# The recurrence's block-diagonal gate products: float32r in three passes instead of fp32

## The chip, the cores and the metric

The kernel runs on one NeuronCore of a Trainium2 chip. The metric is the device time of one execution in microseconds (us). The engines are named as the profile names them: PE (TensorE, matrix products; PEld is its loading of weights), DVE (VectorE), ACT (ScalarE), POOL (GpSimd) and SP (SyncE, which here issues DMA transfers). Lower is better.

## The reference, cut to what matters

The program is one inference step of a decoder layer on 264 tokens: 256 of a prompt and 8 single tokens of running sequences. A combined projection `xn @ w_in` feeds two groups of heads: a gated linear recurrence (RG-LRU) and an mLSTM. Then come an output projection, cross attention over 256 memory tokens, and a SwiGLU feed-forward part. The part that this document is about is the pair of gates of the recurrence:

```python
xr, conv_new = causal_conv(z[..., OFF_RGX:OFF_RGG], conv_buf, conv_w, conv_b)
r = jax.nn.sigmoid(block_diag(xr, w_rg_a, b_rg_a))
ig = jax.nn.sigmoid(block_diag(xr, w_rg_x, b_rg_x))
h_rg, h_last = rglru(xr, r, ig, rg_lambda, h0)
```

`xr` has 1024 channels in 8 blocks of 128. `block_diag` multiplies each block by a 128 x 128 matrix of its own, once for `r` and once for `ig`: 16 products of 128 x 128 by 128 x 264. From `r` and `ig` come the coefficients of a first-order recurrence over the 256 prompt tokens.

## The kernel before, in words

Activations lie transposed: channels on the 128 partitions, the 264 tokens along the free dimension. All large projections are a list of **steps** (`steps`, lines 164 and 1478). A step of the main kind takes one 128-column piece of a weight matrix (2048 rows, as 16 blocks of 128 x 128) and makes one 128 x 264 output in a PSUM bank.

**Three float32r passes.** Precision is kept by splitting each operand into a high part, rounded to float32r, and a low part, the rest. `mm3` (line 287) makes a product of three float32r passes: high by high, high by low, low by high. The moving operand is read in an order that interleaves its two halves (`turn`), and the result is read back the same way (`unturn`, `halves`). A step is so 16 x 3 = 48 passes. The weights are split while the kernel runs (`split_half`, line 183): a DMA on SP's queue brings half a step's weights (128 x 1024) into one of 5 `raw` tiles, ACT makes the high part, DVE subtracts it to make the low part, both into one of 4 `w` tiles, that is two steps' worth. These splits have a high priority.

**The order of the work.** Steps 0 to 3 are the first four projections of the recurrence's input, worked row by row; 4 to 7 the other four; 8 a narrow one for the mLSTM's gates (32 passes); 9 to 24 the mLSTM's q, k and v; 25 to 32 the recurrence's output gate; 33 to 40 the mLSTM's. Beside the list, **generators** make the work of the heads. After each step `pump` (line 323) lets each generator run until DVE's or ACT's clock, by the kernel's own prices, is ahead of PE's; `yield STEP` ends a generator's turn until the next step. What is issued so gets its priority from its place in the program, and a scheduler then orders each engine's queue by priority and by the time at which it reckons an operand ready; PE is ordered by hand only for steps 0 to 6 and at the end. Each engine works through its queue in that order.

**The recurrence's generator** is `rg_gen` (line 528), started at step 7. It loads the 16 gate matrices (two DMAs on SP's queue, 512 KB each), computes the decay's coefficients (`rg_coef`), and takes the 8 blocks in turn: `rg_conv(n)` (line 512) makes the causal convolution, one ACT instruction and three DVE instructions of some 256 to 296 columns and one short one. After every second block the generator ends its turn, and at its next it issues for both blocks the two gate products, in fp32, each followed by a sigmoid on ACT that reads the PSUM bank:

```python
            for q in (n - 1, n):
                for t, j, b in ((r, 0, "ba"), (ig, 1, "bx")):
                    ps = bank("ax")
                    pe.matmul(ps[:, :N], wr[j][:, q, :], rg["xr"](q), start=True, stop=True)
                    last = act.activation(t(q), ps[:, :N], AF.Sigmoid, bias=V(b, q))
```

Then come exponentials and square roots on ACT, multiplications and eight scans on DVE. Step 25 is not issued until `rg_gen` is through.

**Tiles.** Most intermediate tiles come from one pool of 26 slots (`B`, line 119): the normalized input (8 slots until step 40), the convolution's inputs, gate matrices, `xr`, `r`, `ig`, the mLSTM's tiles and loaded states.

**POOL** is used before the change for a few memsets, for DMA issue, and, in the cross attention, for low parts of 256 columns (lines 1202 and 1256).

Of the kernel before, what the change touches and what calls it, by code (L numbers as in the profile page):

```python
# [10 lines left out]
F32 = mybir.dt.float32  # L11
F32R = mybir.dt.float32r
I32 = mybir.dt.int32
AF = mybir.ActivationFunctionType
# [3 lines left out]
P = 128  # L18
# [4 lines left out]
N = T + NS  # L23
# [19 lines left out]
STEP = object()  # L43
# [52 lines left out]
def layer_kernel(ctx: ExitStack, tc, xT, memT, vec, wrg, w_in, w_out, w_q, w_k, w_v, w_o,  # L96
# [3 lines left out]
    act, dve, pe = Engine(nc.scalar, price_act), Engine(nc.vector, price_dve), Engine(nc.tensor, price_pe)  # L100
    pool_e, sp = nc.gpsimd, nc.sync
# [13 lines left out]
    def nm(s):  # L115
        uid[0] += 1
        return f"{s}_{uid[0]}"

    def B(shape, dt=F32):
        return sb.tile(shape, dt, tag="B", bufs=NB, name=nm("B"))  # L120

    def tmp(w=N, tag="t"):
        t = sb.tile([P, N], F32, tag=tag, bufs=NT if tag == "t" else NL, name=nm(tag))
        return t[:, :w]
# [146 lines left out]
    def by2(x):  # L271

        return x.rearrange("p (a b) -> p a b", b=2)

    def turn(x):

        return x.rearrange("p (b a) -> p a b", b=2)

    def halves(x):

        return x.rearrange("p (b a) -> p b a", b=2)

    def unturn(ps):

        return ps.rearrange("p (a b) -> p b a", b=2)

    def mm3(ps, a, b, start, stop):
        ah, al = a
        bh, bl = b
        ps, bh, bl = by2(ps), turn(bh), turn(bl)  # L290
        pe.matmul(ps, ah, bh, start=start, stop=False)
        pe.matmul(ps, ah, bl, start=False, stop=False)
        pe.matmul(ps, al, bh, start=False, stop=stop)
# [53 lines left out]
    def bank(tag="mm"):  # L347
        return psm.tile([P, 512], F32, tag=tag, bufs=4, name=nm(tag))
# [16 lines left out]
    def V(name, j=0, w=1):  # L365
        o = _V[name][0] + j
        return vecs[:, o: o + w]
# [87 lines left out]
    rg = {"zn": 0}  # L455

    def rg_coef():

        c = const.tile([P, 2 * RGB], F32, name="rgc")
        lam = V("lam", 0, 8)  # L460
        n_ = tmp(8)
        with tc.issue_after(st["low"].ins):
            dve.scalar_tensor_tensor(n_, lam, -1.0, lam, op0=OP.mult, op1=OP.min)
        e = tmp(8)
        act.activation(e, n_, AF.Exp)
        l1 = tmp(8)
        log1p(l1, e)
        m = tmp(8)
        dve.tensor_scalar(m, lam, -1.0, 0.0, op0=OP.mult, op1=OP.max)
        dve.tensor_add(m, m, l1)  # L470
        dve.tensor_scalar(c[:, :8], m, -8.0, None, op0=OP.mult)
        dve.tensor_scalar(c[:, 8:], m, -16.0, None, op0=OP.mult)
        rg["c"] = c

    def log1p(out, e):

        w = e.shape[-1]
        pp = e.shape[0]
        s = ctile(w)[:pp]
        q = ctile(w)[:pp]  # L480
        dve.tensor_scalar(q, e, 2.0, None, op0=OP.add)
        dve.reciprocal(q, q)
        dve.tensor_mul(s, e, q)
        s2 = ctile(w)[:pp]
        dve.tensor_mul(s2, s, s)
        dve.tensor_scalar(q, s2, 1.0 / 19, None, op0=OP.mult)
        for k in (17, 15, 13, 11, 9, 7, 5, 3):
            dve.scalar_tensor_tensor(q, q, 1.0 / k, s2, op0=OP.add, op1=OP.mult)
        dve.scalar_tensor_tensor(out, q, 1.0, s, op0=OP.add, op1=OP.mult)
        dve.tensor_scalar(out, out, 2.0, None, op0=OP.mult)  # L490
# [21 lines left out]
    def rg_conv(n):  # L512
        z = rg.pop(("z", n))
        zi, t = z[:, 0, :], z[:, 1, :]
        smp = zi[:, 267:299].rearrange("p (b j) -> p b j", j=4)
        act.activation(cpo[:, n, :], zi[:, 256:259], AF.Copy)
        act.activation(cso[:, n, :, :], smp[:, :, 1:4], AF.Copy)
        w = [V("cw", j * 8 + n) for j in range(4)]
        act.activation(t[:, :296], zi[:, 0:296], AF.Identity, scale=w[0], bias=V("cb", n))
        dve.scalar_tensor_tensor(t[:, :296], zi[:, 1:297], w[1], t[:, :296], op0=OP.mult, op1=OP.add)  # L520
        dve.scalar_tensor_tensor(t[:, :296], zi[:, 2:298], w[2], t[:, :296], op0=OP.mult, op1=OP.add)
        xr = rg["xr"](n)
        dve.scalar_tensor_tensor(xr[:, :T], zi[:, 3:259], w[3], t[:, :T], op0=OP.mult, op1=OP.add)
        ts = t[:, 267:299].rearrange("p (b j) -> p b j", j=4)
        dve.scalar_tensor_tensor(xr[:, T:N].rearrange("p (b j) -> p b j", j=1), smp[:, :, 3:4], w[3],
                                 ts[:, :, 0:1], op0=OP.mult, op1=OP.add)

    def rg_gen():
        wr = [B([P, 8, P]), B([P, 8, P])]
        for j in range(2):  # L530
            sp.dma_start(wr[j], wrg[:, j * 8: j * 8 + 8, :])
        rg_coef()
        r, ig = Arr(RGB), Arr(RGB)
        for n in range(RGB):
            while rg["zn"] <= n:
                yield STEP
            rg_conv(n)
            yield 1.5
            if n % 2 == 0:
                continue  # L540
            yield STEP
            for q in (n - 1, n):
                for t, j, b in ((r, 0, "ba"), (ig, 1, "bx")):
                    ps = bank("ax")
                    pe.matmul(ps[:, :N], wr[j][:, q, :], rg["xr"](q), start=True, stop=True)
                    last = act.activation(t(q), ps[:, :N], AF.Sigmoid, bias=V(b, q))
            yield 0.1
        yield STEP
        xr, c = rg["xr"], rg["c"]
        e2 = Arr(RGB)  # L550

        for n in range(RGB):
            with tc.issue_after(last.ins), tc.issue_after(st["split"].ins):
                act.activation(e2(n), r(n), AF.Exp, scale=c[:, 8 + n: 9 + n])
                le = act.activation(r(n), r(n), AF.Exp, scale=c[:, n: n + 1])
                act.activation(e2(n), e2(n), AF.Relu, scale=-1.0, bias=ones[:, 0:1])
            dve.tensor_mul(ig(n), ig(n), xr(n))
            yield 0.8
        for n in range(RGB):
            with tc.issue_after(le.ins), tc.issue_after(st["split"].ins):  # L560
                act.activation(e2(n), e2(n), AF.Sqrt)
            dve.tensor_mul(ig(n), ig(n), e2(n))
            yield 0.4
        h = Arr(RGB)
        rg["h"] = h
        for n in range(RGB):
            dve.tensor_tensor_scan(h(n)[:, :T], r(n)[:, :T], ig(n)[:, :T], 0.0, op0=OP.mult, op1=OP.add)
            yield 0.6
        h0 = V("h0", 0, 64).rearrange("p (n b) -> p n b", b=NS)
        for q in range(2):  # L570
            hq, rq_, iq = (t.tile(q)[:, :, T:N] for t in (h, r, ig))
            dve.tensor_mul(hq, rq_, h0[:, 4 * q: 4 * q + 4, :])
            dve.tensor_add(hq, hq, iq)
            act.activation(hlast[:, 4 * q: 4 * q + 4, :], h.tile(q)[:, :, T - 1: N], AF.Copy)
        yield 0.3
# [902 lines left out]
    for i, (src, cols, pef, evf, need) in enumerate(steps):  # L1478
        if i > 1:
            load_piece(i + LD - 1)  # L1480
        if i == 7:
            st["rg"] = side(rg_gen(), 0)
# [20 lines left out]
        ps = pef(i)  # L1503
# [148 lines left out]
```

## Time and profile before

| | |
|---|---|
| median of 3 runs | 1439.19 us (1438.92 to 1440.05) |
| the profiled execution | 1438.81 us, of it the span of the profile 1437.1 us |
| PE busy | 1425.1 us, 99% of the span |
| DVE, ACT, POOL busy | 1039.0, 804.1, 125.5 us (72%, 56%, 9%) |
| granted TensorE clock, mean | 0.999 |

A row of the timeline reads: start and length in us, engine, line, operation, output tile `<-` input tiles, shapes, number of instructions merged in the row; in brackets the idle time before it and what ended that. A row of a group (by line, engine, operation and tiles) ends with the number of instructions, their busy time in us and the mean of one in ns, and the idle time of the engine before them. Lengths of PE instructions hold the time of the pipeline, so that following ones overlap. Where a helper issues an instruction, its line is the helper's (L61): the tiles tell what it is. `w<-raw,w` on DVE is the low part of the main weights, `w<-raw` on ACT the high part, `mm<-B,w` on PE a pass of a main step, `ax<-B,B` with 264 columns a gate product of the recurrence. A row of the windows gives for a stretch its length and the busy time, with the number of instructions, of PE, PEld, DVE, ACT and POOL, then the granted clock, the DMA share and GB/s. A row of waits reads: who waited for whom, us in total, times, longest.

### The profile page before, as it was taken

What the parts mean: (1) busy time and instruction counts of PE and PEld (TensorE: products, weight loads), DVE (VectorE), ACT (ScalarE), POOL (GpSimd) and SP (SyncE); (2) the same over time, 40 slices, a digit from 0 to 9 for tenths busy, and PEclk for the clock granted to TensorE, in tenths of its full rate; (3) what the DMA queues carried; (4) which work ended last, traced back from release to release, by engine and by line L of the source; (5) the groups of instructions that cost most, each with busy time, mean ns of one, the idle gap of its engine ahead of it and who ended that gap; (6) DMA issues with size and microseconds to landing.
All of it is one profiled execution on the core that took longest, in us unless ns stands there. A gap on an engine that the chain in (4) does not pass through costs nothing.

```text
span 1437.1 us, 29866 instructions
## 1 busy us (share of the span) xinstructions
PE 1425.1 (99%) x11959; PEld 1403.2 (98%) x11959; DVE 1039.0 (72%) x1972; ACT 804.1 (56%) x1290; POOL 125.5 (9%) x195
## 2 busy tenths in 40 slices
PE   9999999999999999999999999999999999999997
PEld 9999999999998999999999999999999999999997
DVE  7957898997899999977666655555656655566565
ACT  7778876775556666665544444334444433444474
POOL 0000220000224434400000000000000000000000
PEclk9999999999999999999999999999999999999999
DMA  9755898557899887846555555555555555555573
GB/s 301 241 185 188 295 364 288 185 193 254 290 332 396 300 331 270 323 164 216 193 190 197 200 191 195 199 193 194 200 195 192 198 197 192 196 197 193 165 241 127
DMA packets 98140, 329.16 MB, mean 229 GB/s; under 512 B 10865, under 2 KB 17441, under 8 KB 98001
## 3 DMA queue, kind: packets, MB, share of 16 engines
q1 hardware_dynamic: 81840, 271.96, 54.4%
q0 software_dynamic: 15296, 54.21, 10.3%
q8 instruction: 93, 1.52, 0.4%
q10 hardware_dynamic: 864, 1.08, 0.2%
q14 instruction: 47, 0.38, 0.1%
HBM read 314.36 MB, written 12.86 MB: 228 GB/s over the span
## 4 chain that ended last, share of the span: by engine, by line
PE 69%; DVE 1%; issue 0%; ACT 0%; POOL 0%; DVEq 0%; POOLq 0%; ACTq 0%
PE mm L61 67%; PE ax L61 2%; DVE B L61 0%; DVE w L61 0%; DVE dw L61 0%; POOL ds L1202 0%; DVE t L61 0%; ACT w L61 0%; ACT t L61 0%; DVE ax L61 0%; ACT dw L61 0%; ACT ds L61 0%; DVE rstd L61 0%; DVE osm L61 0%; DVEq L1629 0%
## 5 line engine op out<-in xcount | busy, mean ns | idle before, releaser
L61 PE MATMUL mm<-B,w 128*128 128x264 f32 (+1 forms) x10960 | 1281.5, 279 | 0.0
L61 PEld LDWEIGHTS mm<-B,w 128*128 128x128 f32 x10960 | 1261.4, 189 | 7.6
L61 DVE TENSOR_TENSOR w<-raw,w 128x1024 fp32r<-128x1024 f32 (+1 forms) x506 | 613.5, 1214 | 303.3 <-ACT w L61 302.7
L61 ACT ACTIVATE w<-raw 128x1024 fp32r<-128x1024 f32 (+1 forms) x506 | 525.5, 1042 | 497.1 <-PE mm L61 344.6
L61 PE MATMUL mm<-w,B 128*128 128x512 f32 x384 | 86.5, 380 | 0.0
L61 PEld LDWEIGHTS mm<-w,B 128*128 128x128 f32 x384 | 70.7, 189 | 9.4
L1543 POOL TENSOR_TENSOR B<-B,rstd 128x264 f32<-128x264 f32 x4 | 2.9, 747 | 801.9 <-ACT B L61 801.9
L61 DVE TENSOR_TENSOR t<-mm,rstd 128x264 f32<-128x264 f32 x96 | 41.6, 433 | 28.8 <-PE mm L61 28.7
L61 DVE SCALAR_TENSOR_TENSOR B<-B,dw 128x256 f32<-128x256 f32 x128 | 53.7, 473 | 2.8 <-ACT dw L61 2.7
L61 DVE TENSOR_TENSOR xres<-xres,mm 128x264 f32<-128x264 f32 (+1 forms) x81 | 34.1, 424 | 24.9 <-PE mm L61 24.9
L61 DVE SCALAR_TENSOR_TENSOR dw<-B,qsm,dw 128x256 f32<-128x256 f32 x96 | 48.1, 507 | 0.7
L1202 POOL TENSOR_TENSOR ds<-dw,ds 128x256 fp32r<-128x256 f32 x32 | 36.6, 1145 | 105.4 <-ACT ds L61 105.3
L61 PE MATMUL ax<-B,B 128*128 128x256 f32 (+3 forms) x276 | 43.8, 301 | 0.7 <-DVE B L61 0.7
L61 PEld LDWEIGHTS ax<-B,B 128*128 128x128 f32 x276 | 37.9, 191 | 2.9 <-DVE B L61 1.0
L61 ACT ACTIVATE B<-xres,vecs 128x264 fp32r<-128x264 f32 (+1 forms) x64 | 32.4, 506 | 10.3 <-DVE xres L61 8.3
L61 ACT ACT_TABLE_LOAD x21 | 26.9, 1283 | 4.1 <-issue 2.2
L1191 POOL DMA_DIRECT2D B<-kcT x32 | 17.3, 541 | 131.1 <-DVE B L61 118.0
L61 ACT ACTIVATE dw<-B,qsm 128x256 f32<-128x256 f32 x32 | 16.3, 508 | 19.3 <-issue 9.7
L61 ACT ACTIVATE t<-xres 128x264 f32<-128x264 f32 (+1 forms) x46 | 18.8, 410 | 14.0 <-DVE xres L61 13.9
L61 ACT ACTIVATE B<-t 128x264 fp32r<-128x264 f32 (+1 forms) x60 | 24.2, 410 | 1.8 <-DVE t L61 1.8
L61 ACT ACTIVATE dw<-ax,dw 128x256 f32<-128x256 f32 x32 | 15.0, 470 | 17.5 <-DVE dw L61 16.6
L61 ACT ACTIVATE ds<-dw 128x256 fp32r<-128x256 f32 x32 | 13.3, 416 | 19.9 <-DVE dw L61 19.8
(176 smaller groups left out, 700.3 us busy)
## 6 DMA issues: line engine op xcount, KB each, us to landing
raw<-w_gu SPq DMA_DIRECT2D x176, 512.0 KB, 3.6
raw<-w_d SPq DMA_DIRECT2D x80, 512.0 KB, 3.7
raw<-w_in SPq DMA_DIRECT2D x74, 512.0 KB, 5.1
raw<-w_out SPq DMA_DIRECT2D x32, 512.0 KB, 3.9
raw<-w_q SPq DMA_DIRECT2D x32, 512.0 KB, 4.9
B<-kcT POOLq DMA_DIRECT2D x32, 512.0 KB, 8.2
B<-vcT POOLq DMA_DIRECT2D x32, 512.0 KB, 9.8
raw<-w_k SPq DMA_DIRECT2D x32, 512.0 KB, 5.2
```

What stands on the lines that cost most here:

```text
L61: return f(*a, **k)
L1191: pool_e.dma_start(kc, kcT[h, b])
L1202: pool_e.tensor_sub(ws[:, 1], acc, ws[:, 0].bitcast(F32))
L1543: e.tensor_mul(st["y"](c), st["y"](c), r)
```

## The change

The gate products are made by `mm3`, so both operands are split. After `rg_coef` the generator ends its turn. At the next one it makes of each of the two loaded tiles of gate matrices (128 x 1024) a high part on ACT and a low part on POOL (`pool_e.tensor_sub`), in four new tiles of the pool. After each second block, ACT makes the high part of both blocks' `xr` (128 x 528) in a new tile, POOL the low part, the turn ends, and at the next turn the products follow, 12 passes for two blocks. The sigmoid reads the result with its halves interleaved, as the three passes leave it. The convolutions, the exponentials, the scans and all else are as before.

```diff
         rg_coef()
+        yield STEP
+        wr2 = []
+        for j in range(2):
+            wh, wl = B([P, 8, P], F32R), B([P, 8, P], F32R)
+            act.activation(wh, wr[j], AF.Copy)
+            pool_e.tensor_sub(wl, wr[j], wh.bitcast(F32))
+            wr2.append((wh, wl))
+            yield 1.1
         r, ig = Arr(RGB), Arr(RGB)
...
             if n % 2 == 0:
                 continue
+            x2, o = B([P, 2, 2, N], F32R), (n - 1) % 4
+            x = rg["xr"].tile(n // 4)[:, o: o + 2, :]
+            act.activation(x2[:, 0], x, AF.Copy)
+            pool_e.tensor_sub(x2[:, 1], x, x2[:, 0].bitcast(F32))
+            yield 0.6
             yield STEP
             for q in (n - 1, n):
                 for t, j, b in ((r, 0, "ba"), (ig, 1, "bx")):
                     ps = bank("ax")
-                    pe.matmul(ps[:, :N], wr[j][:, q, :], rg["xr"](q), start=True, stop=True)
-                    last = act.activation(t(q), ps[:, :N], AF.Sigmoid, bias=V(b, q))
+                    mm3(ps[:, :N], tuple(w[:, q, :] for w in wr2[j]),
+                        (x2[:, 0, q - n + 1], x2[:, 1, q - n + 1]), True, True)
+                    last = act.activation(halves(t(q)), unturn(ps[:, :N]), AF.Sigmoid, bias=V(b, q))
```

## The prediction

> **What bounds the kernel now.** I read the page's busy times and its chain first, then the PE timeline around the products that change, then the two engines beside it.
>
> ```profile
> span 1437.1 us, 29866 instructions
> PE 1425.1 (99%) x11959; PEld 1403.2 (98%) x11959; DVE 1039.0 (72%) x1972; ACT 804.1 (56%) x1290; POOL 125.5 (9%) x195
> 716.10 707.41 PE mm L61 x6288
> PE ax L61 <- DVE B L61: 0.7, 1, 0.7
> ```
>
> PE (TensorE) is busy 99% of the span. The third row, from the chain of waits in order of time, is 6288 float32r products on end, so one takes 707.41 / 6288 = 0.1125 us. The last row is PE's wait list from 30 to 1420 us: a single idle wait of 0.7 us. So a product less is time saved only if PE's operands stay on time, and any operand that is late adds its lateness in full. The profiled execution took 1438.81 us (span 1437.1 and 1.7 around it); the median of the runs is 1439.19, 0.38 above. The sum is made against 1438.81 and 0.38 added at the end.
>
> The changed products in the PE timeline, four groups of four:
>
> ```profile
> 54.41 1.96 PE L61 MATMUL ax<-B,B 128*128 128x264 f32 x8
> 56.01 10.93 PE L61 MATMUL mm<-B,w 128*128 128x264 f32 x94
> 66.78 0.73 PE L61 MATMUL ax<-ident,B 128*128 128x4 f32 x6
> 67.37 5.65 PE L61 MATMUL mm<-B,w 128*128 128x264 f32 x48
> 72.85 1.94 PE L61 MATMUL ax<-B,B 128*128 128x264 f32 x8
> 86.19 1.94 PE L61 MATMUL ax<-B,B 128*128 128x264 f32 x8
> 99.44 1.94 PE L61 MATMUL ax<-B,B 128*128 128x264 f32 x8
> L61 PE MATMUL ax<-B,B 128*128 128x264 f32 x32 | 7.8, 387 | 0.0
> ```
>
> An fp32 product has two records. In a row of 1.94 us the last record shows its own 0.387 us, so the seven before it take (1.94 - 0.387) / 7 = 0.222 us each, a product 0.444 us.
>
> VectorE (DVE) and GpSimd (POOL) in that stretch, and later where both work:
>
> ```profile
> 36.00:72.00 36.00, 36.00 (x313) 35.57 (x312) 35.86 (x95) 26.13 (x58) 0.00 (x0) 1.00 0.74 242
> 72.00:108.00 36.00, 36.00 (x299) 34.97 (x298) 20.35 (x44) 26.66 (x43) 1.79 (x3) 1.00 0.52 183
> 440.00:460.00 20.00, 20.00 (x112) 18.01 (x111) 19.90 (x39) 13.91 (x24) 12.18 (x18) 1.00 1.01 382
> ```
>
> The columns are PE, PEld, DVE, ACT, POOL. From 36 to 72 us DVE is busy 35.86 of 36 us: it carries the convolutions of the recurrence and the low parts of the main weights together, with nothing to spare, while POOL does nothing. From 72 us DVE has 15.65 us of slack in 36.
>
> **The products themselves.** Removed: 32 records, 32 x 0.222 = 7.10 us. Added: 16 x 3 = 48 float32r products, 48 x 0.1125 = 5.40 us, with the same interleaved moving operand and 128 columns of weights as the main ones. PE gains 1.70 us. That is all the change can gain, and it is 0.12%: a measurement of this kernel tells about 0.2% (2.9 us) from no change.
>
> **ScalarE.** It makes two weight high parts of 1024 columns and four input high parts of 528.
>
> ```profile
> L61 ACT ACTIVATE w<-raw 128x1024 fp32r<-128x1024 f32 x488 | 514.3, 1057 | 490.4 <-PE mm L61 337.9 <-issue 124.0 <-ACT t L61 15.5
> L61 ACT ACTIVATE w<-raw 128x512 fp32r<-128x512 f32 x18 | 11.3, 630 | 6.6 <-PE mm L61 6.6
> ```
>
> 2 x 1.06 + 4 x 0.63 = 4.6 us, against 36 - 26.13 = 9.9 us that ACT has idle from 36 to 72 us. I put it at nothing; without that cover the pieces would push the weight splits behind them, by up to 4.6 us in all. The sigmoid now reads and writes in interleaved halves of the same 264 columns; same answer.
>
> **Moved.** The weights' load keeps its place in SP's queue. The new stops of the generator move the convolutions a step back in the order of issue and the first group of products some two steps, so the recurrence's chain ends later.
>
> ```profile
> 133.44 0.69 DVE L61 TENSOR_TENSOR_SCAN B<-B,B 128x256 f32<-128x256 f32 x1
> 161.36 5.75 PE L61 MATMUL mm<-B,w 128*128 128x264 f32 x48
> 84.49 0.70 POOL L689 DMA_DIRECT2D o_m<-mrow  x1 [60.52 <-DVE mrow L61]
> ```
>
> Its last scan ends at 134.1 us, and it has to be through before the products of 161.36 (the first that its result gates): 27 us of cover for two steps of 5.4 us. I put that at nothing; if the chain slipped further, PE would wait for the excess over 27 us. In POOL's queue the nearest other work is the store at 84.49 us and the state loads behind it; 12 us of subtractions from 53 us on are through before it, and if one stood behind that store, a group of products would wait for 84 us.
>
> **GpSimd's low parts: the term that decides.** Two of 1024 columns and four of 528, 4160 columns. What POOL takes, and what it does to DVE:
>
> ```profile
> L1202 POOL TENSOR_TENSOR ds<-dw,ds x32: 723/1161/1742, 363.3 to 608.3; 128x256 fp32r<-128x256 f32 x32
> 396.06 0.41 DVE L61 SCALAR_TENSOR_TENSOR B<-B,dw 128x256 f32<-128x256 f32 x1
> 396.41 1.16 DVE L61 SCALAR_TENSOR_TENSOR B<-B,dw 128x256 f32<-128x256 f32 x1
> 396.54 0.74 POOL L1202 TENSOR_TENSOR ds<-dw,ds 128x256 fp32r<-128x256 f32 x1
> 546.30 0.95 DVE L61 SCALAR_TENSOR_TENSOR B<-B,dw 128x256 f32<-128x256 f32 x1
> 545.20 2.64 POOL L1256 TENSOR_TENSOR B<-t,B 128x256 fp32r<-128x256 f32 x3
> ```
>
> The same DVE instruction takes 0.41 us alone and 1.16 us when a POOL subtraction of 0.74 us starts beside it: it ends only after POOL's end. Where three POOL subtractions run on end, each DVE instruction takes 0.95, 0.54 more. POOL's own time goes from 0.72 to 1.74 the other way round. The two engines hold each other up while both read two operands from SBUF. So work on POOL is not free of DVE: it costs DVE 0.54 us (0.95 - 0.41) to 0.74 us (POOL's whole instruction) per 256 columns when DVE is busy, 8.8 to 12.0 us for 4160 columns, and nothing when DVE is idle.
>
> The Trainium skill speaks against the change here (SBUF — State Buffer, Who interferes with whom): a DVE instruction with two SBUF inputs contends with a GpSimd instruction that reads SBUF, and whoever issues first keeps the pair for the whole instruction. The trace agrees that they collide; by that rule every piece would cost its whole length, the wait worked out below would be 7.5 us and the time 1445.0, where the back-to-back rows show 0.54 of 0.74.
>
> What is behind it in DVE's queue: the low parts of the main weights, which PE needs.
>
> ```profile
> 54.38 1.06 DVE L61 SCALAR_TENSOR_TENSOR B<-B,vecs 128x296 f32<-128x296 f32 x3
> 55.35 1.23 DVE L61 TENSOR_TENSOR w<-raw,w 128x1024 fp32r<-128x1024 f32 x1
> 57.00 1.23 DVE L61 TENSOR_TENSOR w<-raw,w 128x1024 fp32r<-128x1024 f32 x1
> 58.57 1.23 DVE L61 TENSOR_TENSOR w<-raw,w 128x1024 fp32r<-128x1024 f32 x1
> 63.49 2.24 DVE L61 SCALAR_TENSOR_TENSOR B<-B,vecs 128x256 f32<-128x256 f32 x8
> 65.72 1.22 DVE L61 TENSOR_TENSOR w<-raw,w 128x1024 fp32r<-128x1024 f32 x1
> 66.93 1.22 DVE L61 TENSOR_TENSOR w<-raw,w 128x1024 fp32r<-128x1024 f32 x1
> DMA to landing us min/median/max: 6.3/6.7/7.1
> L531 SPq DMA_DIRECT2D B<-wrg x2: 425/428/432, 47.2 to 47.7; - x2
> ```
>
> A step is 48 products (5.4 us), a half step 2.7 us, and the third product of a half needs its low part. The group at 54.41 stands behind the first two products of a step; the 22 others of that half follow at 56.2, so the next half starts at 58.66 and needs its low part at 58.9. It is ready at 55.35 + 1.23 = 56.6: slack 2.3 us. The halves after it need theirs at 61.6 and 64.3 and have them at 58.2 and 59.8 (slack 3.4 and 4.5); the second half of the step of 67.37 needs its at 70.3 and has it at 66.9 (3.4); the next needs 74.9, has 68.15 (6.7). With the change the first group (1.78 us) is no longer ahead of these halves, and PE comes earlier: slack 0.5, 1.6, 2.7; then, with the new group (1.35 us) in between, 3.0; then, with the second group gone too, 4.5.
>
> The weights land at 47.2 + 6.3 and 47.7 + 7.1 = 53.5 and 54.8 us, so POOL's two long pieces and the first input piece fall right into 53 to 65 us. Until the fifth half above, two long and two short pieces have run: 3104 columns, 6.5 to 9.0 us of DVE; minus 3.0, PE waits 3.5 to 6.0 us. Until the last, all six: 8.8 to 12.0 minus 4.5, 4.3 to 7.5 us. DVE has no idle time there to give back. PE's loss is the largest of these, not their sum: 3.5 to 7.5 us, less if part of POOL's work falls behind 72 us. I take 4.8, nearer the lower end, because the rows with back-to-back work (0.54) are nearest to a saturated DVE.
>
> Sum: 1438.81 - 1.70 + 4.8 = 1441.9; with 0.38, **1442.3 us**, 0.2% slower. Its own range is a wait of 2.5 to 7.5 us: 1440.0 to 1445.0.
>
> **Rivals.** (1) Not slower: the cover holds. POOL's pieces are issued behind DVE's full stretch, or the low parts of the main weights stand ahead of the convolutions in DVE's queue, and the lateness at each half stays under 0.5 to 4.5 us. For it: from 440 to 460 us POOL works 12.18 us and DVE 19.90 of 20, and PE still has no idle time. Against: there the pieces have 256 columns, and the stretch is not one that begins with slack 0.5. Then the 1.70 us remain: 1437.5. It turns to the forecast when POOL delays DVE by more than 2.7 us before about 64 us.
>
> (2) PE waits for POOL itself. The first group is due behind the step that ends at 66.78 - 1.78 = 65.0. The chain is landing 54.8, high part 1.06, two long pieces and one short one on POOL. At 0.74 per 256 that is 7.4 us, ready at 63.3, no wait; at the median 1.161 it is 11.7, ready at 67.6, 2.6 us late; at 1.742 it is 17.5, 8.4 us late. A wait of 2.6 alone gives 1440.1, of 8.4 alone 1445.9. It isn't added to the forecast: the later of the two counts.
>
> (3) The order shifts further on. The recurrence's chain comes two steps later and meets the work around 155 us where PE had its one wait of 0.7 us; the four new tiles take slots of the pool of 26.
>
> ```profile
> POOL B L857 <- PE ax L61: 21.7, 1, 21.7
> DVE B L61 <- ACT B L61: 4.6, 4, 2.8
> ```
>
> POOL waits 21.7 us there for a slot as it is. That wait can shrink or a step can slip by half, 2.7 us: 1437.5 - 0.7 = 1436.8 up to 1440.2.
>
> **How the numbers follow.** Forecast 0.46, (1) 0.34, (2) 0.10, (3) 0.10. Slower by over 0.2% (above 1442.1): 0.30 of the forecast, 0.06 of (2), 0.04 of (3): 0.40. Faster by over 0.2% (below 1436.3) is more than any of these prices gives; I leave it 0.04 of (1) and 0.03 of (3), for small waits of the stretch that no view lists and that a new order could remove: 0.07. Within 0.2%: 0.53. Range 1437.0 to 1446.0: from just under (1) to the long wait of (2).
>
> **What would show it.** Products right: 48 records at 0.1125 us each in four groups of 1.35 us. Forecast right: DVE subtractions w<-raw,w of 1.7 us and more between 53 and 72 us, overlapping POOL pieces of 2.5 to 4 us, and PE or PEld idle with DVE w as releaser in 57 to 75 us. (1) right: no PE wait there, and DVE's full stretch only a little longer. (2) right: the releaser is POOL B. Wrong in the basis: POOL's 1024 columns not near four times 0.72 us, or DVE not lengthened beside them.

## The result, and the profile after

| | before | after |
|---|---|---|
| median of the runs | 1439.15 us (1438.92 to 1440.05, 4 runs) | 1455.96 us (1454.08 to 1458.43, 4 runs) |
| the profiled execution | 1438.81 us, span 1437.1 us | 1458.43 us, span 1456.7 us |

After is **1.0118** times as long as before, 95% interval 1.0106 to 1.013: 1.2% slower, 16.8 us. The forecast was 1442.3 us, in a range up to 1446.0.

The head of the page of after; its last row is the granted clock in 40 slices:

```profile
span 1456.7 us, 29920 instructions
PE 1432.7 (98%) x11975; PEld 1410.2 (97%) x11975; DVE 1047.4 (72%) x1972; ACT 805.7 (55%) x1296; POOL 136.0 (9%) x201
...
PEclk9999999899999999999999999999999999999999
```

PE's instructions are 16 more, as they should be (48 for 32). Yet its busy time rose by 7.6 us, and one slice of the clock, near 255 to 290 us, shows an 8. Where the time goes is seen by laying the main passes of the two traces side by side (every product that writes an `mm` bank, counted from 0): how much later does the pass of the same number start in after?

```
main pass no.        100    300    400    700   1200   1700   1950   3000   last
starts before, us  32.59  57.33  69.25 109.78 179.49 236.65 266.75 386.42 1426.67
later in after, us  0.60  -1.20   7.40   6.78   5.92   5.65   20.52  20.09   20.07
```

The loss comes in **two places**: some 6 us between 57 and 70 us, and 14.4 us (20.1 - 5.6) between 240 and 267 us, by the times of before. Behind them nothing more is lost. (The profiled execution of after is the longest of its four, 2.5 us above their median, so the two places sum to more than the 16.8 us of the medians.) The windows of the two places, first of before, then of after (columns: length, then busy time and instructions of PE, PEld, DVE, ACT, POOL, then the granted clock, the DMA share, GB/s):

```profile
54.00:76.00 22.00, 22.00 (x183) 21.38 (x182) 21.31 (x66) 14.85 (x23) 0.00 (x0) 1.00 0.67 228
255.00:295.00 40.00, 40.00 (x357) 39.95 (x356) 35.98 (x72) 29.65 (x56) 0.00 (x0) 1.00 0.53 185
```

```profile
54.00:76.00 22.00, 17.76 (x128) 17.17 (x127) 19.14 (x39) 11.83 (x16) 8.85 (x5) 0.84 0.54 184
255.00:295.00 40.00, 31.43 (x228) 29.98 (x227) 28.51 (x80) 19.70 (x41) 0.53 (x1) 0.87 0.45 174
```

PE idles 22.00 - 17.76 = 4.24 us in the first window and 8.57 us in the second, and in both the clock granted falls well below 1.

**The first place.** PE's timeline of after:

```profile
58.87 2.97 PE L61 MATMUL mm<-B,w 128*128 128x264 f32 x24 [1.00 <-DVE w L61]
62.88 0.38 PE L61 MATMUL ax<-B,B 128*128 128x264 f32 x1 [1.03 <-ACT B L61]
65.46 8.31 PE L61 MATMUL mm<-B,w 128*128 128x264 f32 x46 [2.21 <-DVE w L61]
73.61 1.40 PE L61 MATMUL ax<-B,B 128*128 128x264 f32 x11
```

Three waits, 1.00 + 1.03 + 2.21 = 4.24 us: twice for the low part of a main weight, once for the high part of the first input pair, which itself waits for a convolution on DVE. Then come 46 passes in 8.31 us: up to 71.3 us they start 0.22 us apart in place of 0.1125. These 27 slow passes cost 27 x 0.1075 = 2.9 us. Together 7.1 us; less the 1.70 us that the products save, 5.4, and 5.65 was measured at pass 1700.

What held DVE, from the timelines of DVE, POOL and ACT of after:

```profile
56.26 2.56 DVE L61 TENSOR_TENSOR w<-raw,w 128x1024 fp32r<-128x1024 f32 x1 [1.88 <-ACT w L61]
58.74 2.33 DVE L61 TENSOR_TENSOR c<-c 128x8 f32<-128x8 f32 x1
60.99 3.28 DVE L61 SCALAR_TENSOR_TENSOR B<-B,vecs 128x256 f32<-128x256 f32 x8
...
55.37 5.68 POOL L538 TENSOR_TENSOR B<-B,B 128x1024 fp32r<-128x1024 f32 x2 [39.38 <-ACT B L61]
62.90 1.34 POOL L552 TENSOR_TENSOR B<-B,B 128x528 fp32r<-128x528 f32 x1
...
54.22 1.06 ACT L61 ACTIVATE B<-B 128x1024 fp32r<-128x1024 f32 x1 [2.41 <-DMA B<-wrg]
```

POOL's two long subtractions run from 55.37 to 61.05; singly they take 2.37 and 3.35 us (2371 and 3348 ns are the shortest and longest of line 538). A subtraction of 1024 columns on DVE, started beside the first, ends 1.1 us behind it and takes 2.56 us; alone it takes 1.22. An instruction of 8 columns, started during the second, ends with it, after 2.33 us; alone it takes 0.16. With the eight short ones beside the third piece (3.28 against 2.24 in the row that the prediction shows) DVE loses 1.34 + 2.17 + 1.04 = 4.6 us. The last row is a second suspect: ACT's copy of the gate matrices stands in ACT's queue and waits 2.41 us for its load, and DVE waits 1.88 us for a copy behind it.

**The second place.** To read it one has to know three generators that the prediction did not look at. `ml_sample` makes the mLSTM's state products, piece by piece, and stores them (`o_sc`). When it is through, `ml_norm` can start: two products with `ssum`, a long chain of short DVE instructions, transposes on PE, and at its end an operand of the output projection. In step 42, the second of that projection, the program lets all generators run until the norm is through, whatever the clocks say. `mem_gen` loads and squares the memory tokens from step 40 on. Before, on POOL, PE and DVE:

```profile
203.16 0.53 POOL L917 DMA_DIRECT2D o_sc<-B  x1 [5.84 <-DVE ds L61]
...
239.80 0.33 PE L61 MATMUL ax<-ssum,ones 128*128 128x64 f32 x2
256.66 1.47 PE L61 MATMUL ax<-ident,B 128*128 128x128 f32 x12
257.89 29.72 PE L61 MATMUL mm<-B,w 128*128 128x264 f32 x262
...
256.80 0.89 DVE L61 SCALAR_TENSOR_TENSOR B<-B,vecs,B 128x264 fp32r<-128x264 f32 x2
```

From `ssum` to the first pass with the norm's result there are 257.89 - 239.80 = 18.1 us, and DVE makes the low part of its operand from 256.80 on: the chain was just in time, with less than 1 us to spare. After, on POOL, PE and ACT:

```profile
244.19 0.53 POOL L931 DMA_DIRECT2D o_sc<-B  x1 [30.64 <-DVE ds L61]
...
258.94 0.33 PE L61 MATMUL ax<-ssum,ones 128*128 128x64 f32 x2
263.23 0.49 PE L61 MATMUL mm<-B,w 128*128 128x264 f32 x2 [1.20 <-ACT w L61]
264.49 2.74 PE L61 MATMUL mm<-B,w 128*128 128x264 f32 x22 [0.77 <-DVE w L61]
270.27 0.81 PE L61 MATMUL mm<-B,w 128*128 128x264 f32 x2 [3.04 <-ACT w L61]
271.53 4.99 PE L61 MATMUL mm<-B,w 128*128 128x264 f32 x22 [0.45 <-DVE w L61]
279.40 3.73 PE L61 MATMUL ax<-ident,B 128*128 128x128 f32 x16 [2.87 <-DVE B L61]
284.24 16.02 PE L61 MATMUL mm<-B,w 128*128 128x264 f32 x140 [0.23 <-DVE B L61]
...
260.90 0.42 ACT L61 ACTIVATE lt<-B 128x256 f32<-128x256 f32 x1 [2.62 <-DMA B<-memT]
```

The last state store is 41 us later, `ssum` 19.1 us. PE itself is 5.6 us late there, so the chain starts 13.5 us later than PE's work needs it, and PE loses 14.4 us: 8.57 in waits, and most of the rest in work at a low clock (22 passes in 4.99 us that took 2.74 just before). The 13.5 us are a matter of order alone: `ssum` stands behind 1728 main passes in PE's queue before and behind 1848 after, and 120 x 0.1125 = 13.5. The last row shows how the memory's work joins in: ACT waits 2.62 us for its load, and a high part of the main weights stands behind it.

### The profile page after: what moved, and what is told of

Read it like the earlier page. It is cut to its first block, busy times and chain, and to the rows that moved or that the text cites. A ratio compares the mean times of both kernels' runs of the same rounds, so it can differ in the third digit from the quotient of the medians.

```text
span 1456.7 us, 29920 instructions
## 1 busy us (share of the span) xinstructions
PE 1432.7 (98%) x11975; PEld 1410.2 (97%) x11975; DVE 1047.4 (72%) x1972; ACT 805.7 (55%) x1296; POOL 136.0 (9%) x201
## 4 chain that ended last, share of the span: by engine, by line
PE 68%; DVE 1%; issue 0%; ACT 0%; POOL 0%; DVEq 0%; POOLq 0%; ACTq 0%
PE mm L61 66%; PE ax L61 2%; DVE B L61 0%; DVE w L61 0%; DVE dw L61 0%; POOL ds L1216 0%; DVE t L61 0%; ACT w L61 0%; ACT t L61 0%; DVE ax L61 0%; ACT dw L61 0%; ACT ds L61 0%; DVE rstd L61 0%; DVE osm L61 0%; DVEq L1643 0%
## 5 line engine op out<-in xcount | busy, mean ns | idle before, releaser
L61 ACT ACTIVATE dw<-B,qsm 128x256 f32<-128x256 f32 x32 | 16.2, 507 | 22.7 <-issue 10.6
L61 ACT ACTIVATE B<-B 128x264 f32<-128x264 f32 (+7 forms) x43 | 22.5, 535 | 9.7 <-DVE B L61 7.2
L61 ACT ACTIVATE dw<-ax,dw 128x256 f32<-128x256 f32 x32 | 15.0, 470 | 19.1 <-DVE dw L61 13.0
```

What stands on the lines that cost most here:

```text
L61: return f(*a, **k)
```

## The experiments

Two theories. **Collision**: GpSimd's subtractions hold VectorE back, and all else follows from that. **Order**: the new stop alone moves the recurrence, and with it all generators behind it, so that the norm at step 42 comes late. Each kernel is compared with before as it was timed beside it.

### The stop alone, with fp32 products

```diff
         rg_coef()
+        yield STEP
+        for j in range(2):
+            yield 1.1
...
                 continue
+            yield 0.6
             yield STEP
```

> The kernel before, with its fp32 gate products, and only the changed kernel's pauses put into the recurrence's generator: the one stop behind the coefficients and the three pauses; no split, nothing on GpSimd. By the order theory (the stop alone moves the recurrence two steps on, the state products end 40 us later, and TensorE pays 14 us at 255 to 290 us) it takes 1439.2 + 14 = about 1453 us, with memT's loads near 249 us, and hardly anything lost at 55 to 75 us. By the rival theory (all the loss comes from GpSimd's subtractions and ACT's extra copies, and the late part is their echo) it takes 1439 to 1440 us.

1452.53 us against 1439.36, ratio 1.0088 (1.0072 to 1.0105): 13 us slower without a single split. PE's timeline of this kernel:

```profile
251.92 0.33 PE L61 MATMUL ax<-ssum,ones 128*128 128x64 f32 x2
262.00 0.55 PE L61 MATMUL mm<-B,w 128*128 128x264 f32 x2 [4.21 <-ACT w L61]
274.31 17.93 PE L61 MATMUL mm<-B,w 128*128 128x264 f32 x157 [1.63 <-DVE B L61]
```

The late place is there, with nothing lost before it (PE is 1.4 us early at pass 1700). The order theory holds for the larger part of the loss. (The profiled execution was the fastest of this kernel, 1448.85 us, 3.7 us under its median: its rows show the place and not the whole price.)

### The stop taken out, and GpSimd taken out

```diff
         rg_coef()
-        yield STEP
         wr2 = []
```

> The changed kernel without the stop behind the coefficients; splits, GpSimd and float32r passes stay. By the order theory the recurrence ends at its old step, memT's loads go back to about 210 us and the 14 us at 255 to 290 us are gone. The early loss tells two causes apart: if it is ACT's queue standing behind a weight copy that waits for the load of the gate matrices, it grows from 6 us to 8 to 10 (the copy now stands a step earlier in the queue while the load still lands near 54 us), and the time is 1437.5 + 9 = 1446 us; if it is the collision of GpSimd with VectorE alone, it stays near 6 us, 1443 us.

```diff
-            pool_e.tensor_sub(wl, wr[j], wh.bitcast(F32))
+            nc.vector.tensor_sub(wl, wr[j], wh.bitcast(F32))
...
-            pool_e.tensor_sub(x2[:, 1], x, x2[:, 0].bitcast(F32))
+            nc.vector.tensor_sub(x2[:, 1], x, x2[:, 0].bitcast(F32))
```

> The changed kernel with all low parts made on VectorE in place of GpSimd, at the same places of the program. If the collision on the shared operands of GpSimd and VectorE makes the early loss (the forecast's step), the loss at 55 to 75 us falls from 6 us to 1 or 2 and the time to about 1451 us. If ACT's queue behind the late load makes it, the loss stays at 4 to 6 us and the time at 1454 to 1457 us. The 14 us at 255 to 290 us stay by either, since the order is kept.

And both at once:

> The kernel without the stop, with all low parts on VectorE: both suspected causes taken away at once. If the loss is the sum of the two (6 us early from GpSimd's reads, 14 us late from the stop), what is left is the products' gain of 1.7 us less 0 to 2 us from VectorE's own 4.7 us of extra subtractions: 1437.5 to 1439.5 us. If ACT's weight copy waiting for its load (2.7 us) also costs, 1440 to 1443 us.

| | with the stop | without it |
|---|---|---|
| low parts on GpSimd | 1455.96 (the change) | 1446.08, 1.0043 (1.0028 to 1.0058) |
| low parts on VectorE | 1451.15, 1.0077 (1.0062 to 1.0092) | 1440.56, 1.0007 (0.9998 to 1.0015) |

(Before took 1439.15 us beside the changed kernel, 1439.69 beside the one with neither cause, 1439.36 beside the other two.) The two causes add up: the stop costs 9.9 us with GpSimd and 10.6 without, GpSimd 4.8 us with the stop and 5.5 without. With fp32 products the stop cost 13.2 us; why some 3 us more is not shown. The windows show each in its own place; first the kernel without the stop, then the one with all low parts on VectorE:

```profile
54.00:76.00 22.00, 16.52 (x141) 15.77 (x140) 20.25 (x39) 15.22 (x25) 14.75 (x8) 1.00 0.46 152
255.00:295.00 40.00, 40.00 (x358) 39.97 (x357) 37.70 (x87) 27.30 (x50) 0.00 (x0) 1.00 0.57 182
```

```profile
54.00:76.00 22.00, 21.30 (x185) 20.71 (x184) 20.89 (x44) 17.03 (x26) 0.00 (x0) 1.00 0.62 207
255.00:295.00 40.00, 32.72 (x253) 31.61 (x252) 33.13 (x91) 22.26 (x42) 0.00 (x0) 0.91 0.44 152
```

Without the stop the late place is full again, and PE still idles 5.48 us in the early one. With VectorE it is the other way round. On VectorE a low part is cheap and delays nobody by more than itself:

```profile
55.26 1.23 DVE L538 TENSOR_TENSOR B<-B,B 128x1024 fp32r<-128x1024 f32 x1 [1.11 <-ACT B L61]
56.40 1.22 DVE L61 TENSOR_TENSOR w<-raw,w 128x1024 fp32r<-128x1024 f32 x1
57.54 0.16 DVE L61 TENSOR_TENSOR c<-c 128x8 f32<-128x8 f32 x1
```

1.23 us in place of GpSimd's 2.37 and 3.35, and the instruction of 8 columns takes 0.16 in place of 2.33. The second suspect, ACT's copy waiting for its load, is left in the kernel with neither cause. All that PE waits there, from 30 to 1420 us, for ACT's splits of main weights and for DVE's:

```profile
PE mm L61 <- ACT w L61: 0.4, 1, 0.4
PE mm L61 <- DVE w L61: 0.8, 1, 0.8
```

So its waits cost 0.4 us by themselves, and 1.2 us if the wait for DVE is its doing too. The kernel without the stop came out at the 1446 that the expectation gave to this suspect, but not by its way: PE is 5.4 us late after the early place, not 8 to 10, and 1.9 us more near 203 us, with one wait of 1.4 for a main low part, whose cause stays open. The kernel with neither, at 1440.56, missed the range for the sum of the two causes by 1.1 us; it lies in the range that was given to ACT's copy. The products' gain of 1.7 us does not show, and the 1.2 us of waits above explain only a part of that; copy and DVE's own extra subtractions were not separated.

### Which GpSimd pieces

Without the stop, first only the inputs' low parts left on GpSimd, then only the gate matrices':

> The kernel without the stop; the two 1024-column low parts of the gate matrices on VectorE, the four 528-column low parts of the inputs stay on GpSimd. If the loss of 6 us at 55 to 75 us comes mainly from the two long pieces, which hold VectorE's next instruction for up to 2.8 us each, 1438 to 1441 us; if every column costs alike, 2112 of 4160 columns keep half of it, 1441 to 1443 us.

> The other half: the two 1024-column low parts on GpSimd, the four 528-column ones on VectorE, no stop. Long pieces to blame: 1443 to 1446 us, near the kernel without the stop. Every column alike: 1441 to 1443 us.

1441.29 us (1.001, 1.0001 to 1.0019) and 1442.86 us (1.0024, 1.0015 to 1.0033), against 1439.69. Against the kernel with neither (1440.56) the short pieces cost 0.7 us, the long ones 2.3, though both halves have nearly equal columns (2112 and 2048). Both medians lie within the 1441 to 1443 us expected if every column costs alike, so by the ranges the long pieces are not to blame alone. But 0.7 against 2.3 us is not alike either, and the long ones fall where DVE is full; length and place are not told apart. The two halves give only 3.0 of the 5.5 us: the rest is there only when both stand in the same stretch.

### The memory branch later

```diff
-        if i == 40:
+        if i == 44:
             st["memg"] = side(mem_gen(), 7)
```

> The changed kernel, with one number altered: the memory branch joins the side work after step 44 instead of step 40, so that its loads and squares no longer run inside the forced ending of the mLSTM's norm at step 42. By the order theory the loss at 255 to 290 us falls from 14 us to 0 to 3, and the time from 1456 to 1442 to 1445 us; the 6 us lost at 55 to 75 us stay. By the rival theory that the 14 us are a slow clock or late weights that follow from the early loss, it stays at 1454 to 1457 us.

1450.66 us (1.0074, 1.0059 to 1.0089). Only 5.3 us of the 14 came back, so the expectation missed. The rest is the norm's own lateness, seen in PE's timeline:

```profile
257.95 0.33 PE L61 MATMUL ax<-ssum,ones 128*128 128x64 f32 x2
...
274.43 17.80 PE L61 MATMUL mm<-B,w 128*128 128x264 f32 x141 [2.59 <-DVE B L61]
```

`ssum` is nearly as late as in after. From there to the pass that waits for DVE's low part of the norm's result, the chain takes 16.5 us where nothing else is forced beside it, and 284.24 - 258.94 = 25.3 in after, where the memory's work is forced in the same step. In the traces the two share the late loss about equally (7.7 us are left of 14.4).

### Starting the recurrence a step earlier

The kernel with the stop and all low parts on VectorE, with `if i == 6` for `if i == 7` at the start of the generator.

> The changed kernel with its stop, low parts on VectorE, and the recurrence's generator started after step 6 instead of 7, so that the gate matrices are loaded and split a step earlier than in the changed kernel. If the late loss comes from the recurrence itself ending late, it is gone: 1438 to 1441 us. If what counts is the step at which the planner has written the last state product (step 36 in the kernel before, 39 in the changed one, 37 here, by counting the planner's steps) against the norm that is forced at step 42, a part of the 14 us stays: 1441 to 1448 us, with PE waits between 255 and 290 us.

1447.47 us (1.0055, 1.0041 to 1.0068). It is inside the second range, but not for the expected reason alone: PE had lost 8.6 us by pass 1700, in waits spread over 50 to 215 us, and 2.1 us in the late place. Loading and splitting earlier moved the trouble into other steps. As a test of the late place it helps all the same, as one more dose. (The state products end after planner step 37 in before, 40 in the changed kernel and 38 here; the expectation counts them one lower.) For seven kernels, in us, from the starts of `ssum` and of the main passes in the profiled executions (which are up to 4 us off the medians):

```
                         ssum later  PE late at   chain later      lost after
                         than before  pass 1700   than PE needs    pass 1700
the change                  19.15       5.65          13.5            14.4
stop alone, fp32            12.12      -1.38          13.5            11.5
stop, lows on VectorE       12.50      -1.00          13.5            11.7
memory branch at 44         18.16       4.66          13.5             7.7
started at step 6           13.96       8.56           5.4             2.1
no stop                      7.26       7.26           0               0
no stop, lows on VectorE     0.62       0.62           0              -0.4
```

The four kernels with the stop at the old start have the same 13.5 us, whatever their products and their early loss: `ssum` stands behind 1848 main passes in all four, behind 1776 in the one started at step 6, and behind 1728 in every kernel without the stop, as before. Where it is 0, nothing is lost.

### The products in the old order

The float32r products put into before with no stop and no pause, the splits not counted in the planner's clocks, the gate matrices split only when the first pair is due, all low parts on VectorE, the products and the sigmoid as in the change; then the same with the first input pair split ahead of the gate matrices.

```diff
                 continue
+            if n == 1:
+                for j in range(2):
+                    wh, wl = B([P, 8, P], F32R), B([P, 8, P], F32R)
+                    nc.scalar.activation(wh, wr[j], AF.Copy)
+                    nc.vector.tensor_sub(wl, wr[j], wh.bitcast(F32))
+                    wr2.append((wh, wl))
+            x2, o = B([P, 2, 2, N], F32R), (n - 1) % 4
+            x = rg["xr"].tile(n // 4)[:, o: o + 2, :]
+            nc.scalar.activation(x2[:, 0], x, AF.Copy)
+            nc.vector.tensor_sub(x2[:, 1], x, x2[:, 0].bitcast(F32))
             yield STEP
```

> The float32r products put into the kernel before so that the order of everything else stays as it was: no stop and no pause, the splits not counted in the planner's clocks, the gate matrices split only ahead of the first group of products (so that ACT's copy no longer stands before convolutions while its load is on the way), all low parts on VectorE. If the products' gain of 1.7 us can be had at all, 1437.5 us, faster than the kernel before; if VectorE's full stretch at 36 to 72 us takes 1 to 2 us back, 1438.5 to 1439.5 us, no change.

> As the version that kept the order, but with the first input pair split ahead of the gate matrices, so that ScalarE's high part of the input no longer stands behind two weight copies of 1.06 us. If that queue made TensorE's wait of 1.4 us at the first group, the time falls by 1 to 1.4 us, to 1438.3 to 1438.8 us, and 1.0 to 1.4 us below the kernel before; if VectorE's convolution was late itself, it stays at 1439.7.

1439.74 us against 1439.69, ratio 1.0003 (0.9994 to 1.0012), no change; and 1441.64 against 1439.79, 1.0011 (1.0002 to 1.002). The first lies just above its second range; the second lies outside both of its own: it did not help, it cost. The longest row of PE's wait list, of the first and of the second, and then a row of the second's ACT timeline:

```profile
PE ax L61 <- ACT B L550: 1.4, 1, 1.4
```

```profile
PE mm L61 <- ACT w L61: 1.7, 1, 1.7
```

```profile
54.38 1.06 ACT L549 ACTIVATE B<-B 128x1024 fp32r<-128x1024 f32 x1 [1.88 <-DMA B<-wrg]
```

In the first, PE waits 1.4 us for the first input pair, about what the products save. In the second that wait is gone, and a main weight split of ACT is 1.7 us late instead, behind the copy that waits for its load. So the gain of 1.7 us was not to be had in either order; no version tried beats the kernel before.

## Why the prediction was wrong

**Bounds and products: right.** PE was the bound, and lateness counted in full, at a low clock even for more. The group row of the gate products in after, 50 to 120 us, and one group of twelve:

```profile
L61 PE MATMUL ax<-B,B 128*128 128x264 f32 x48 | 6.3, 278 | 1.0 <-ACT B L61 1.0
86.32 1.51 PE L61 MATMUL ax<-B,B 128*128 128x264 f32 x12
```

48 records, (1.51 - 0.278) / 11 = 0.112 us each: the 1.70 us are there.

**Moved: the step that failed.** The prediction gave the stop two steps' delay, looked where the recurrence's result is needed (161.36 us), found 27 us of cover and wrote "I put that at nothing". For the recurrence that was right: no wait there in any kernel. But the generators behind it draw on the same budget of the planner. The state products came to their end three planner steps later, and what hangs on them, the norm that is forced at step 42, had less than 1 us of cover. That is 14.4 us of the 20 lost in the profiled execution, put at 0; taken out alone, the stop is worth 9.9 to 10.6 us of the median. The rows that would have told it stand in the profile of before: `ssum` at 239.80 and its operand at 256.80 for a pass at 257.89.

**GpSimd's low parts: mechanism and place right, price short.** Forecast: PE waits 4.8 us for low parts of main weights at 57 to 75 us. Measured: 4.24 us of waits there, 3.2 of them for DVE's main low parts, DVE's instructions lengthened beside POOL's long pieces (2.37 and 3.35 us, on average 2.84 = 3.9 x 0.72, as assumed). Missing in the sum were the 27 passes at half rate, 2.9 us. Taken out alone, GpSimd is worth 4.8 to 5.5 us. The delay of DVE was less than stated (4.6 us where 6.5 to 9.0 were given for the first 3104 columns, of which the last 528 came only at 77.70 us), but less of the slack was left too, since DVE also waited 1.88 us for ACT.

**ScalarE at nothing: nearly right**, but a cost was overlooked: not the copies' 4.6 us but the wait of the first for its load, 2.41 us in the queue. With neither of the two causes PE waits 0.4 us for ACT's splits, and 0.8 for DVE's; whether the 0.8 come from this copy is not shown.

**The rivals.** (1), cover holds: refuted, the lateness passed the 0.5 to 4.5 us of slack. (2), PE waiting for POOL itself: no such wait in the list of after. The one wait of a gate product, 1.03 us, was for ACT, whose copy waited for DVE. (3), the order shifts further on: the right kind of cause with the wrong place and price. It looked at 155 us, where PE in fact loses nothing, and gave it 1436.8 to 1440.2; the place was 100 us later and the price 10 to 14 us.

Without the stop, the kernel that the forecast's sum really describes took 1446.1 us, 3.8 above the forecast: no half rate there, but 5.48 us of idle time where 4.8 were taken, the 1.9 us near 203 us, and the rest mostly in small waits up to 160 us.

## What to carry to other kernels

A stop in one generator is a change to everything that is planned behind it: follow the shift to the next point where work is forced to end, and ask there how early the operand was, not only at the moved result. Take a VectorE that is full as a reason against GpSimd work with two SBUF operands beside it: here the same subtractions were cheaper on VectorE itself. And price a wait of a bound TensorE above its length when two waits stand close together.

## What the runs showed of the hardware

**The clock after waits.** In after, PE made one product between 61.84 and 65.46 us. The granted clock in that stretch:

```profile
62.00:64.00 2.00, 0.38 (x1) 0.19 (x1) 2.00 (x6) 1.79 (x3) 1.97 (x2) 1.00 0.04 14
64.00:66.00 2.00, 0.54 (x2) 0.54 (x3) 2.00 (x4) 1.13 (x2) 0.24 (x1) 0.63 0.00 0
66.00:68.00 2.00, 2.00 (x11) 2.00 (x10) 2.00 (x4) 0.00 (x0) 0.00 (x0) 0.50 0.69 217
```

Where 1.00 turns into 0.50, a mean of 0.63 over 2 us means (1 - 0.63) / 0.5 x 2 = 1.5 us at the lower rate: the clock fell near 64.5 us, while PE still waited; 27 passes then ran at 0.22 us, just half rate, up to 71.3 us. In the kernel without the stop PE idled longer in the window of 22 us (5.48 us against 4.24), but between 61.1 and 65.41 us it made six products, and the granted clock stayed at 1.00. So what is done inside some 3 to 4 us seems to count, not the sum of the waits; where the limit lies was not measured. The Trainium skill (TensorE: Matmul & The Clock Gate, Part 1: The HAM clock gate) says that the clock is either full or half, and that it is halved after an idle window of about 3.4 us. The half rate agrees. But none of the three waits of 1.00, 1.03 and 2.21 us is that long, and the stretch with one product in it had lasted only 2.7 us when the clock fell; here a stretch that was nearly, not wholly, idle was enough.

**A lock, seen on a tiny instruction.** A DVE instruction of 8 columns took 2.33 us because it started beside a POOL piece of 3.35 us, and 0.16 us in the kernel with all low parts on VectorE. By the Trainium skill (SBUF — State Buffer, Who interferes with whom) the engine that issues first keeps the pair of SBUF ports that the two share for its whole instruction; the row agrees. In these rows a POOL piece so costs DVE the time until POOL is through, whether DVE's instruction has 8 columns or 1024.
